# A hybrid attention block on one Trainium2 core: the last inverse softmax sums through TensorE and PSUM, and another order of the first loads

## The chip, the core and the metric

The kernel runs on one core of one Trainium2 chip. The core has five engines that run beside each other, each in the order of its own list of instructions: TensorE (PE) for matmuls, with a row of its own for weight loads (PEld); VectorE (DVE) and ScalarE (ACT) for work on tiles; GpSimd (POOL); and SyncE (SP), which here only issues DMA transfers. ACT and POOL issue transfers too. The metric is the time of one execution on the device in microseconds (us), lower is better.

## What is computed

The reference is one decoder block in float32 with 512 tokens of width 1024. Two attention branches of 8 heads of 64 read the same normalised input through one projection.

```python
h = rms_norm(x, norm_g[layer])
proj = h @ w_in[layer]
fq, fk, fv, fz, mq, mk, mv, mz, ga, gb, fl = split_cols(proj, IN_SPLITS)
...
log_f = jax.nn.log_sigmoid((fl + b_f[layer]).astype(jnp.float32)).transpose(0, 2, 1)
y_fox = from_heads(fox_attention(q, k, v, log_f)) * jax.nn.silu(fz)
...
y_moba = from_heads(moba_attention(q, k, v)) * jax.nn.silu(mz)
merged = (jax.nn.sigmoid(ga + b_gate[layer, 0]) * (y_fox @ w_fox[layer])
          + jax.nn.sigmoid(gb + b_gate[layer, 1]) * (y_moba @ w_moba[layer]))
x = x + merged @ w_out[layer]
```

The first branch (f, "fox") is causal softmax attention with a forget term in its logits. The second (m, "moba") has rotary positions and is causal too; with 512 tokens in blocks of 256 its choice of blocks leaves out nothing. Each softmax divides by a sum over the keys, and this kernel does so at the end of a head, by multiplying the head's output with the inverse of the sum.

## The kernel before, in words

**Precision.** Every matrix is split into a high part and a low part, both of a type that PE takes at its fast pace, and a product is three matmuls: high x high, high x low, low x high. ACT makes the high part by a copy, and DVE makes the low part by a subtraction. For a weight piece this is `split` (L107 to L113: `wh_...` on ACT at L110, `wl_...` on DVE at L112).

**Start.** `load_g` (L96 to L103) loads one of the eight slices of x transposed (`xt`, 256 KB, on SP's queue) and splits it into `Zh` (ACT, L101) and `Zl` (DVE, L102). `load_quarters` (L124 to L139) loads the first weight chunk `fqa` in quarters of two slices. The first quarter comes as two transfers of one slice each, one on ACT's queue and one on SP's, and is split by two casts (L134) and two subtractions (L137), all on DVE. The constants `cs` (L66) go first on ACT's queue. Eight matmuls on zeros (L82) occupy PE at first. `first_qk` (L350 to L361) then runs over the eight slices with four banks of PSUM, three matmuls for each of four token tiles (L358 to L360), 96 in all for `fqa`. The chunks `fka`, `fza`, `fzb` follow; `x_stats` (L197 to L208) makes the inverse norms `r` on POOL behind the rope tables that POOL builds (L329 to L333), `norm_row` (L213 to L217) spreads them over partitions, and `normalise` (L219 to L224) turns xt into the normalised `Gh` and `Gl`. The chunk `fva` and its evictions (L319, L320) are the first users of these.

**Attention.** Four groups of four heads run (`attn_group`, L483 to L633), the last one for branch m, half b. For each head: logits and softmax numerators (L530 to L535), transposes of these into `p_a`, `p_b`, `p_cc` (L576), their split (`pth` on ACT L582, `ptl` on DVE L583), then the products with the values into `pv` (L586, L587) and the assembly of two heads into `ypair` (L611, L612). For each pair of heads, `inverse_sums` (L548 to L550) takes the reciprocals `ri` (tokens on partitions), and `sums_out` (L552 to L558) transposes them on PE, copies them on ACT into `rinv_t` and stores them in DRAM; `sums_in` (L560 to L567) loads them back twice, spread over 64 partitions each (`rinv_bc`, on ACT's queue). `Yp` (L619 to L631) multiplies the silu gate `zs` with `rinv_bc` (L626, on POOL, for the very last pair on DVE), the result with `ypair` (L627), and splits it (`yhm` on ACT L628, `ylm` on DVE L629). Projections and other matmuls are laid between the heads as filler.

**Gates.** The gate projections (`group`, L671 to L770) are computed in seven products of half-size matrices in place of eight. Four products read sums of the input that were stored in DRAM and are loaded back by POOL's queue in `load_sums` (L254 to L258, tiles S0 to S3, high and low). Each product has 24 matmuls (L715 to L718); three of its intermediate results are copied out of PSUM by ACT (`e_GA`, L725). Its weights come through four raw buffers and are split by L110 and L112 as above. `GA0` is the first group behind the last attention group, and `yhm` and `ylm` of the last pair are read only later, by `unit_m` (L775 on).

**What sets the order.** The program is written in the order in which work is wanted, and a scheduler fixes the order on each engine before the run. Dependences are kept by tile: an instruction that reads a tile waits for all its writers. Each engine then runs its list in order, and a waiting instruction holds up those behind it.

Of the kernel before, what the change touches and what calls it, by code (L numbers as in the profile page):

```python
# [7 lines left out]
F32 = mybir.dt.float32  # L8
F32R = mybir.dt.float32r
AF = mybir.ActivationFunctionType  # L10
OP = mybir.AluOpType
AX = mybir.AxisListType

P = 128
S = 512
D = 1024
NT = S // P
KT = D // P
HD = 64
CW = 256  # L20
# [3 lines left out]
WR = 4  # L24
# [5 lines left out]
def fox_moba_kernel(ctx: ExitStack, tc, xT, x, w_in, w_fl, w_fox, w_moba, w_out, cst, rope, out):  # L30


    nc = tc.nc
    V, A, G, T = nc.vector, nc.scalar, nc.gpsimd, nc.tensor

    con = ctx.enter_context(tc.tile_pool(name="con", bufs=1))
    sb = ctx.enter_context(tc.tile_pool(name="sb", bufs=1))
# [3 lines left out]
    stage = {}  # L41

    def enter(name):
        if stage:
            stage.pop("guard").__exit__(None, None, None)
        stage["guard"] = tc.tile_pool(name=name, bufs=1, reuse_waits="tile")
        stage["pool"] = stage["guard"].__enter__()

    def t2(tag, bufs, name, shape=(P, 512), dt=F32):
        pool = stage["pool"] if tag in ("qs", "pt", "pc", "ys") else sb  # L50
        return pool.tile(list(shape), dt, name=name, tag=tag, bufs=bufs)

    def pst(tag, bufs, name):
        return ps.tile([P, 512], F32, name=name, tag=tag, bufs=bufs)
# [4 lines left out]
    def tp(name):  # L59
        return pst("tp", 3, name)  # L60


    cs = con.tile([P, C_END], F32, name="cs")
    rp = con.tile([P, NT, 32], F32, name="rp")
    wfl = con.tile([P, KT, 8], F32, name="wfl")
    nc.scalar.dma_start(out=cs, in_=cst)  # L66

    def col(c, n=1):
        return cs[:, c:c + n]

    ident = con.tile([P, P], F32, name="ident")
    triU = con.tile([P, P], F32, name="triU")
    ones = con.tile([P, P], F32, name="ones")
    mask = con.tile([P, 512], F32, name="mask")
    wsc = t2("u", 4, "wsc", (P, 2))
    V.memset(wsc, 0.0)
    A.activation(wsc, wsc, AF.Square)
# [13 lines left out]

    Gh = con.tile([P, KT, S], F32R, name="Gh")
    Gl = con.tile([P, KT, S], F32R, name="Gl")
    XT, Z = {}, {}

    def load_g(*ks):  # L96
        for k in ks:
            xt = XT[k] = t2("y", 15, f"xt{k}")
            nc.sync.dma_start(out=xt, in_=xT[:, k, :])
            zh, zl = Z[k] = [stage["pool"].tile([P, S], F32R, name=f"Z{hl}{k}") for hl in "hl"]  # L100
            A.activation(zh, xt, AF.Copy, scale=col(C_NG + k))  # L101
            V.scalar_tensor_tensor(zl, xt, col(C_NG + k), zh.bitcast(F32), op0=OP.mult, op1=OP.subtract)  # L102


    chunks = {}
# [15 lines left out]
        V.tensor_tensor(out=lo[:, :, CW:264], in0=f, in1=hi[:, :, CW:264].bitcast(F32), op=OP.subtract)  # L121
        chunks.setdefault(name, []).append((hi, lo))

    def load_quarters(name, c0, hf, between):  # L124
        raw = sb.tile([P, 4, CW], F32, name=f"wr_{name}{hf}", tag="wr", bufs=WR)
        hi = sb.tile([P, 4, 264], F32R, name=f"wh_{name}{hf}", tag="wh", bufs=4)
        lo = sb.tile([P, 4, 264], F32R, name=f"wl_{name}{hf}", tag="wl", bufs=4)
        for q in range(2):
            first = hf == 0 and q == 0
            for k in (slice(0, 1), slice(1, 2)) if first else (slice(2 * q, 2 * q + 2),):  # L130
                (nc.scalar if first and k.start == 0 else nc.sync).dma_start(
                    out=raw[:, k], in_=w_in[c0 // CW, :, 4 * hf + k.start:4 * hf + k.stop, :])
                if first:
                    V.tensor_copy(hi[:, k, :CW], raw[:, k])  # L134
                else:
                    A.activation(hi[:, k, :CW], raw[:, k], AF.Copy)
                V.tensor_tensor(out=lo[:, k, :CW], in0=raw[:, k], in1=hi[:, k, :CW].bitcast(F32), op=OP.subtract)  # L137
            load_g(*between[q])
        chunks.setdefault(name, []).append((hi, lo))  # L139

    COLS = {}
    off = 0
# [50 lines left out]
    r = con.tile([P, NT], F32, name="r")  # L193
# [191 lines left out]
    ZS = {}  # L385
# [94 lines left out]
    ri = con.tile([P, 16, 4], F32, name="rinv")  # L480
    R_dram = dr.tile([16, NT, P], F32, name="r_dram")

    def attn_group(br, half, gq, gk):  # L483
        fox = br == "f"
        qn, kn = QN[f"{br}q{half}"], QN[f"{br}k{half}"]
        hb = 4 * (half == "b") + (0 if fox else 8)
        last = br + half == "mb"
        st = {}
# [63 lines left out]
        def sums_out(pr):  # L552
            h0 = hb + 2 * pr
            p = tp("p_ri")
            T.transpose(p[:8, :P], ri[:, h0:h0 + 2, :].rearrange("p h t -> p (h t)"), ident)
            rt = sb.tile([8, P], F32, name="rinv_t", tag="rinv_t", bufs=1)
            A.activation(rt, p[:8, :P], AF.Copy)
            A.dma_start(out=R_dram[h0:h0 + 2].rearrange("h t p -> (h t) p"), in_=rt)  # L558

        def sums_in(pr):  # L560
            if last and pr:
                rb = st["r", pr] = t2("u", 4, "rinv_bc")
            else:
                rb = st["r", pr] = stage["pool"].tile([P, S], F32, name="rinv_bc", tag="rinv_bc", bufs=1)
            for o in range(2):
                A.dma_start(out=rb[o * HD:(o + 1) * HD, :],
                            in_=R_dram[hb + 2 * pr + o].rearrange("t p -> (t p)").partition_broadcast(HD))  # L567

        def Bb(h):
            def go():  # L570
                pts, vt = st[h], VT[f"{br}v{half}"]
                o = h % 2
                pv = pst("pv", 1, "pv")

                def blk(dst, i, j):
                    T.transpose(dst, pts[i][:, j * P:(j + 1) * P], ident)  # L576

                def spl(p, n):
                    tag, w, bufs = ("pt", 512, 4) if n == 512 else ("pc", 256, 2)
                    hi = t2(tag, bufs, "pth", (P, w), F32R)  # L580
                    lo = t2(tag, bufs, "ptl", (P, w), F32R)
                    A.activation(hi[:, :n], p[:, :n], AF.Copy)  # L582
                    V.tensor_tensor(out=lo[:, :n], in0=p[:, :n], in1=hi[:, :n].bitcast(F32), op=OP.subtract)  # L583
                    return hi, lo
                def pvm(j, hl, c0, n, start, stop):
                    T.matmul(pv[:, P * j:P * j + n], vt[:, j, h, :], hl[0][:, c0:c0 + n], start=start, stop=False)  # L586
                    T.matmul(pv[:, P * j:P * j + n], vt[:, j, h, :], hl[1][:, c0:c0 + n], start=False, stop=stop)  # L587
                pa = tp("p_a")
                for i in range(4):
                    blk(pa[:, i * P:(i + 1) * P], i, 0)  # L590
                pb = tp("p_b")
                for i in range(1, 4):
                    blk(pb[:, (i - 1) * P:i * P], i, 1)
                blk(pb[:, 384:512], 3, 3)
                ha = spl(pa, 512)
                hbb = spl(pb, 512)
                pc = tp("p_cc")
                for i in range(2, 4):
                    blk(pc[:, (i - 2) * P:(i - 1) * P], i, 2)
                hc = spl(pc, 256)  # L600
                pvm(0, ha, 0, 512, True, False)
                pvm(1, hbb, 0, 384, False, False)
                pvm(3, hbb, 384, 128, False, False)
                pvm(2, hc, 0, 256, False, True)
                pr = h // 2
                if o == 0:
                    st["y", pr] = t2("u", 4, "ypair") if last and pr else t2("ys", 1, "ypair")
                y = st["y", pr]
                me, ot = (slice(0, HD), slice(HD, P)) if o == 0 else (slice(HD, P), slice(0, HD))
                sh = t2("u", 4, "ysh")  # L610
                A.activation(sh[me, :], pv[ot, :], AF.Copy)  # L611
                V.tensor_tensor(out=y[me, :], in0=pv[me, :], in1=sh[me, :], op=OP.add)  # L612
                if o == 0:
                    sums_out(pr)
                elif pr:
                    sums_in(1)
            return go

        def Yp(pr):  # L619
            def go():  # L620
                y = st["y", pr]
                gp = 2 * (half == "b") + pr
                yh = t2("y", 15, f"yh{br}{gp}", dt=F32R)
                yl = t2("y", 15, f"yl{br}{gp}", dt=F32R)
                zr = st["r", pr]
                (V if (br, gp) == ("m", 3) else G).tensor_tensor(out=zr, in0=ZS[br, gp], in1=zr, op=OP.mult)  # L626
                V.tensor_tensor(out=y, in0=y, in1=zr, op=OP.mult)  # L627
                A.activation(yh, y, AF.Copy)  # L628
                V.tensor_tensor(out=yl, in0=y, in1=yh.bitcast(F32), op=OP.subtract)  # L629
                Y[br, gp] = (yh, yl)  # L630
            return go  # L631
# [239 lines left out]
        for u in filler(names):  # L871
            u()

    enter("start")
    load_g(0)
    load_quarters("fqa", COLS["fqa"], 0, ((1, 2), (3, 4)))
    load_quarters("fqa", COLS["fqa"], 1, ((5, 6), (7,)))
    nc.sync.dma_start(out=wfl, in_=w_fl)
    load_fl("fka", COLS["fka"], 0)
    load_fl("fka", COLS["fka"], 1)  # L880
# [127 lines left out]
```

## Time and profile before

| quantity | value |
|---|---|
| median of 3 runs | 443.63 us (441.45 to 444.06) |
| the profiled execution | 444.28 us |
| its span, first to last instruction | 442.5 us |
| outside the span | 1.78 us |
| mean granted clock of PE | 0.996 |
| instructions | 8082 |
| DMA in all | 56.40 MB, mean 127 GB/s |

The profile is of one execution. Busy time of an engine is the time in which it has an instruction that works; PE's matmuls overlap, so that the time of one is longer than the step from one to the next. A row of the timeline gives start, length, engine, line and operation, and in brackets the idle time before it with what ended it. A chain is followed back from the last instruction, each step to what released it. The costliest groups of the page that lie near the change, with busy time, mean duration in ns and the idle time before:

```profile
L112 DVE TENSOR_TENSOR wl_GA<-wr_ga,wh_GA 128x1024 fp32r<-128x1024 f32 x14 | 16.6, 1219 | 1.2 <-ACT wh_GA L110 1.1
L110 ACT ACTIVATE wh_GA<-wr_ga 128x1024 fp32r<-128x1024 f32 x14 | 14.5, 1054 | 4.5 <-DVE wr_ga L679 2.7
...
L583 DVE TENSOR_TENSOR ptl<-p_a,pth 128x512 fp32r<-128x512 f32 x16 | 11.0, 687 | 5.1 <-ACT pth L582 5.0
```

### The profile page before, as it was taken

The page shows a single profiled execution, that of the slowest core. Times are in us where ns is not written, and L with a number is a line of the kernel's source. Part 1 is how long each engine was busy: PE and PEld are TensorE (multiplying, and loading weights), DVE is VectorE, ACT ScalarE, POOL GpSimd, SP SyncE. Part 2 cuts the span into 40 slices and gives each one's busy share as a digit, 9 for nine tenths or more (in the row PEclk, how much of TensorE's full clock was granted, in tenths as well). Part 3 has the DMA queues.
Part 4 walks back from the last instruction along what each step waited for, and adds up shares of the span by engine and source line. Part 5 has one row for each costly group of instructions (what it writes and reads, how often), then busy time and mean ns, then how long its engine had stood idle before and what let it go on. Part 6 is the DMA issues. An engine that isn't in the chain of part 4 may idle for free.

```text
span 442.5 us, 8082 instructions
## 1 busy us (share of the span) xinstructions
PE 428.4 (97%) x3100; PEld 403.9 (91%) x3100; DVE 314.7 (71%) x563; ACT 262.5 (59%) x491; POOL 87.6 (20%) x106
## 2 busy tenths in 40 slices
PE   6999999999999999999999999987999999999996
PEld 5998899999999998899998878877999989989996
DVE  5559994777998869676956689928978786584311
ACT  5676544876777769887765876717655545531100
POOL 1059200224142950134621002200000000000000
PEclk9999999999999999999999999998999999999999
DMA  8962164424377413303304212663134405624231
GB/s 261 388 246 69 54 205 137 111 74 136 110 233 209 103 55 120 119 13 122 106 14 132 95 24 90 232 203 96 60 133 126 160 1 183 197 96 152 88 96 48
DMA packets 25991, 56.40 MB, mean 127 GB/s; under 512 B 3296, under 2 KB 11936, under 8 KB 25952
## 3 DMA queue, kind: packets, MB, share of 16 engines
q1 hardware_dynamic: 14528, 39.95, 27.4%
q10 hardware_dynamic: 10272, 11.74, 9.0%
q0 software_dynamic: 1152, 4.19, 2.8%
q8 instruction: 24, 0.39, 0.4%
q14 instruction: 15, 0.12, 0.1%
HBM read 46.27 MB, written 6.32 MB: 119 GB/s over the span
## 4 chain that ended last, share of the span: by engine, by line
PE 85%; ACT 6%; DMA 4%; DVE 2%; issue 1%; ACTq 0%; SPq 0%; DVEq 0%
PE pb_GB L718 3%; PE pb_GB L717 3%; PE pb_GB L715 3%; PE po L815 3%; PE po L817 3%; PE po L816 3%; PE pb_GA L715 2%; PE pb_GA L717 2%; PE pb_GA L718 2%; PE pv L587 2%; PE pv L586 2%; PE lg L530 2%; PE lg L531 2%; PE pm L644 2%; PE pm L645 2%; PE pm L646 2%
## 5 line engine op out<-in xcount | busy, mean ns | idle before, releaser
L535 ACT ACTIVATE p<-p,negm 128x128 f32<-128x128 f32 (+1 forms) x64 | 35.7, 558 | 12.5 <-DVE negm L533 11.2
L310 POOL TENSOR_TENSOR ff<-ss,mh 128x8 f32<-128x8 f32 x16 | 27.1, 1699 | 79.6 <-DVE ss L308 77.3
L533 DVE CUSTOM_DVE_ANT_0 p<-lg,mask 128x128 f32<-128x128 f32 (+1 forms) x64 | 30.5, 485 | 5.8 <-PE lg L531 5.6
L815 PE MATMUL po<-wh_wo,mgh 128*128 128x256 f32 x96 | 27.1, 282 | 0.0
L817 PE MATMUL po<-wh_wo,mgl 128*128 128x256 f32 x96 | 27.0, 282 | 0.0
L816 PE MATMUL po<-wl_wo,mgh 128*128 128x256 f32 x96 | 26.9, 281 | 0.0
L825 DVE TENSOR_TENSOR ot<-po,xr 128x256 f32<-128x256 f32 x16 | 6.6, 424 | 24.7 <-PE po L817 23.6
L110 ACT ACTIVATE wh_wo<-wr_wo 128x1024 fp32r<-128x1024 f32 x8 | 8.5, 1061 | 21.6 <-PE po L817 8.0
L530 PE MATMUL lg<-KH,QS 128*128 128x128 f32 (+1 forms) x64 | 20.7, 332 | 0.4 <-DMA KH<-KH 0.4
L112 DVE TENSOR_TENSOR wl_GB<-wr_gb,wh_GB 128x1024 fp32r<-128x1024 f32 x14 | 16.8, 1223 | 4.2 <-ACT wh_GB L110 3.3
L110 ACT ACTIVATE wh_GB<-wr_gb 128x1024 fp32r<-128x1024 f32 x14 | 14.6, 1059 | 8.6 <-PE pm L645 2.5
L612 DVE TENSOR_TENSOR ypair<-pv,ysh 64x512 f32<-64x512 f32 x16 | 11.0, 688 | 10.8 <-ACT ysh L611 10.7
L816 PEld LDWEIGHTS po<-wl_wo,mgh 128*128 128x128 f32 x96 | 18.1, 189 | 0.0
L815 PEld LDWEIGHTS po<-wh_wo,mgh 128*128 128x128 f32 x96 | 18.1, 189 | 0.0
L817 PEld LDWEIGHTS po<-wh_wo,mgl 128*128 128x128 f32 x96 | 18.1, 188 | 0.0
L715 PE MATMUL pb_GA<-Gh,wh_GA 128*128 128x256 f32 x48 | 14.3, 298 | 3.3 <-ACT e_GA L725 3.3
L112 DVE TENSOR_TENSOR wl_GA<-wr_ga,wh_GA 128x1024 fp32r<-128x1024 f32 x14 | 16.6, 1219 | 1.2 <-ACT wh_GA L110 1.1
L110 ACT ACTIVATE wh_GA<-wr_ga 128x1024 fp32r<-128x1024 f32 x14 | 14.5, 1054 | 4.5 <-DVE wr_ga L679 2.7
L504 DVE SCALAR_TENSOR_TENSOR QS<-p_qT,cs,QS 64x512 fp32r<-64x512 f32 x16 | 12.0, 750 | 6.6 <-ACT QS L503 6.2
L611 ACT ACTIVATE ysh<-pv 64x512 f32<-64x512 f32 x16 | 9.5, 593 | 9.8 <-PE pv L587 8.0
L112 DVE TENSOR_TENSOR wl_wo<-wr_wo,wh_wo 128x1024 fp32r<-128x1024 f32 x8 | 9.8, 1222 | 7.4 <-ACT wh_wo L110 7.4
L583 DVE TENSOR_TENSOR ptl<-p_a,pth 128x512 fp32r<-128x512 f32 x16 | 11.0, 687 | 5.1 <-ACT pth L582 5.0
(448 smaller groups left out, 1798.8 us busy)
## 6 DMA issues: line engine op xcount, KB each, us to landing
wr_ga<-in_w_in_dram SPq DMA_DIRECT2D x8, 512.0 KB
wr_gb<-in_w_in_dram SPq DMA_DIRECT2D x8, 512.0 KB
wr_wo<-in_w_out_dram SPq DMA_DIRECT2D x8, 512.0 KB
xt<-in_xT_dram SPq DMA_DIRECT2D x8, 256.0 KB
x<-in_x_dram SPq DMA_DIRECT2D x8, 256.0 KB
s_dramh<-sum_sh ACTq DMA_DIRECT2D x8, 256.0 KB
s_draml<-sum_sl ACTq DMA_DIRECT2D x8, 256.0 KB
KH<-KH ACTq DMA_DIRECT2D x16, 128.0 KB
```

Of the source, the lines that this page charges most:

```text
L110: A.activation(hi[:, :, 0:n], src, AF.Copy)
L112: eng.tensor_tensor(out=lo[:, q, 0:n], in0=src[:, q], in1=hi[:, q, 0:n].bitcast(F32), op=OP.subtract)
L310: G.tensor_tensor(out=f2, in0=ss.rearrange("p t h -> p (t h)"), in1=mh, op=OP.pow)
L530: T.matmul(lg[:, :n], qs[:, qt], kh[:, :n], start=True, stop=False)
L533: V.tensor_tensor_reduce(pt, lg[:, :n], mask[:, 512 - n:512], -0.125, 3.0e38, op0=OP.add, op1=OP.min, accum_out=mkn[:, hh, i:i + 1])
L535: A.activation(pt, pt, AF.Exp, bias=mkn[:, hh, i:i + 1], scale=-1.0, accum_out=rs[:, hh, i:i + 1])
L715: T.matmul(o, hi[:, k, cc], lh, start=(n < 3 and c == 0 and k == 0), stop=False, skip_group_check=True)
L717: T.matmul(o, hi[:, k, cc], ll, start=False, stop=False, skip_group_check=True)
L718: T.matmul(o, lo[:, k, cc], lh, start=False, stop=(k == 3), skip_group_check=True)
L815: T.matmul(p[:, :CW], gh[:, st], hi[:, k, :CW], start=(kk == 0), stop=False)
L816: T.matmul(p[:, :CW], gh[:, st], lo[:, k, :CW], start=False, stop=False)
L817: T.matmul(p[:, :CW], gl[:, st], hi[:, k, :CW], start=False, stop=(kk == KT - 1))
```

## The change

**First loads.** All loads of xt and of `fqa` are issued at the very start by one function. ACT's queue gets xt0 and then cs. SP's queue gets the first two weight slices in one transfer of 256 KB, then xt1, slices 2 and 3 (256 KB), xt2, xt3, slices 4 to 7 (512 KB), xt4 to xt7. `load_g` becomes `split_x` and `load_quarters` becomes `first_split`, which only split. The first quarter is now cast by one instruction of 512 elements a partition, and has one subtraction.

```diff
+    def first_loads():
+        def xt(eng, k):
+            XT[k] = t2("y", 15, f"xt{k}")
+            eng.dma_start(out=XT[k], in_=xT[:, k, :])
+
+        def w(k0, k1):
...
+            nc.sync.dma_start(out=RAW[hf][:, k0 - 4 * hf:k1 - 4 * hf], in_=w_in[0, :, k0:k1, :])
+        xt(nc.scalar, 0)
+        w(0, 2)
+        nc.scalar.dma_start(out=cs, in_=cst)
+        xt(nc.sync, 1)
+        w(2, 4)
+        xt(nc.sync, 2)
+        xt(nc.sync, 3)
+        w(4, 8)
+        for k in range(4, KT):
+            xt(nc.sync, k)
...
+    def first_split(hf, between):
...
         for q in range(2):
...
+            k = slice(2 * q, 2 * q + 2)
+            if hf == 0 and q == 0:
+                V.tensor_copy(hi[:, k, :CW], raw[:, k])
+            else:
+                A.activation(hi[:, k, :CW], raw[:, k], AF.Copy)
+            V.tensor_tensor(out=lo[:, k, :CW], in0=raw[:, k], in1=hi[:, k, :CW].bitcast(F32), op=OP.subtract)
+            split_x(*between[q])
```

**Last inverse sums.** For the very last pair of heads the way through DRAM is left out. POOL writes `ri` into a tile `rinv_w` in which each token's value stands 64 times for each of the two heads, PE transposes it in four steps into a PSUM tile `p_rinv`, and DVE multiplies the gate `zs` with it from there. The other pairs keep their way.

```diff
         def sums_in(pr):
             if last and pr:
-                rb = st["r", pr] = t2("u", 4, "rinv_bc")
...
+                return
...
-                if o == 0:
+                if o == 0 and not (last and pr):
                     sums_out(pr)
...
-                zr = st["r", pr]
-                (V if (br, gp) == ("m", 3) else G).tensor_tensor(out=zr, in0=ZS[br, gp], in1=zr, op=OP.mult)
+                if last and pr:
+                    zr, rb = ZS[br, gp], pst("lg", 2, "p_rinv")
+                    h0 = hb + 2 * pr
+                    rw = t2("u", 4, "rinv_w")
+                    for o in range(2):
+                        G.tensor_copy(rw.rearrange("p (t o d) -> p t o d", o=2, d=HD)[:, :, o, :],
+                                      ri[:, h0 + o, :, None].to_broadcast([P, NT, HD]))
+                    for t in range(NT):
+                        T.transpose(rb[:, t * P:(t + 1) * P], rw[:, t * P:(t + 1) * P], ident)
+                    V.tensor_tensor(out=zr, in0=zr, in1=rb, op=OP.mult)
+                else:
+                    zr = st["r", pr]
+                    G.tensor_tensor(out=zr, in0=ZS[br, gp], in1=zr, op=OP.mult)
                 V.tensor_tensor(out=y, in0=y, in1=zr, op=OP.mult)
```

**The order that the scheduler makes of it.** PE's number of matmuls for `fqa` stays, but for the first slice the products with `Zl` come after the others. In the last attention group, three transposes of the last head's p_a move ahead of the pv group of the head before, p_b and p_cc come right behind that group, and 13 matmuls of GA stand between them and the last pv group. The four transposes into p_rinv stand after 19 of the 24 matmuls of GA's fourth product. On ACT, two wh_GA, e_GA, wh_GA and e_GA now come ahead of yhm; on DVE, zs x p_rinv and the second ypair come behind two wl_GA. POOL makes rinv_w behind the issue of its last S load.

More of the change, by code (lines that the diff above doesn't have):

```diff
@@ L60, in tp @@
         return pst("tp", 3, name)
+    XT, RAW = {}, {}
+    def first_loads():
[3 more added lines that the diff above has]
+        def w(k0, k1):
+            hf = k0 // 4
+            if hf not in RAW:
+                RAW[hf] = sb.tile([P, 4, CW], F32, name=f"wr_fqa{hf}", tag="wr", bufs=WR)
+            nc.sync.dma_start(out=RAW[hf][:, k0 - 4 * hf:k1 - 4 * hf], in_=w_in[0, :, k0:k1, :])
[9 more added lines that the diff above has]
+            xt(nc.sync, k)
     cs = con.tile([P, C_END], F32, name="cs")
@@ L65, in fox_moba_kernel @@
     wfl = con.tile([P, KT, 8], F32, name="wfl")
-    nc.scalar.dma_start(out=cs, in_=cst)
     def col(c, n=1):
@@ L74, in fox_moba_kernel @@
     mask = con.tile([P, 512], F32, name="mask")
+    enter("start")
+    first_loads()
     wsc = t2("u", 4, "wsc", (P, 2))
@@ L93, in fox_moba_kernel, with split_x @@
     Gl = con.tile([P, KT, S], F32R, name="Gl")
-    XT, Z = {}, {}
-    def load_g(*ks):
+    Z = {}
+    def split_x(*ks):
         for k in ks:
-            xt = XT[k] = t2("y", 15, f"xt{k}")
-            nc.sync.dma_start(out=xt, in_=xT[:, k, :])
+            xt = XT[k]
             zh, zl = Z[k] = [stage["pool"].tile([P, S], F32R, name=f"Z{hl}{k}") for hl in "hl"]
@@ L122, in load_fl @@
         chunks.setdefault(name, []).append((hi, lo))
[L124 to L127, printed above, removed]
+    def first_split(hf, between):
+        raw = RAW[hf]
+        hi = sb.tile([P, 4, 264], F32R, name=f"wh_fqa{hf}", tag="wh", bufs=4)
+        lo = sb.tile([P, 4, 264], F32R, name=f"wl_fqa{hf}", tag="wl", bufs=4)
         for q in range(2):
[L129 to L139, printed above, removed]
+            k = slice(2 * q, 2 * q + 2)
[5 more added lines that the diff above has]
+            split_x(*between[q])
+        chunks.setdefault("fqa", []).append((hi, lo))
     COLS = {}
@@ L561, in sums_in @@
             if last and pr:
-                rb = st["r", pr] = t2("u", 4, "rinv_bc")
-            else:
-                rb = st["r", pr] = stage["pool"].tile([P, S], F32, name="rinv_bc", tag="rinv_bc", bufs=1)
+                return
+            rb = st["r", pr] = stage["pool"].tile([P, S], F32, name="rinv_bc", tag="rinv_bc", bufs=1)
             for o in range(2):
@@ L872, in seq @@
             u()
[L874 to L877, printed above, removed]
+    split_x(0)
+    first_split(0, ((1, 2), (3, 4)))
+    first_split(1, ((5, 6), (7,)))
     nc.sync.dma_start(out=wfl, in_=w_fl)
```

## The prediction, made before the changed kernel ran

> **What bounds the kernel now.** I read the page's busy times first, then its chain, then the waits and the chain around the stretches in which TensorE (PE) stands still.
>
> ```profile
> PE 428.4 (97%) x3100; PEld 403.9 (91%) x3100; DVE 314.7 (71%) x563; ACT 262.5 (59%) x491; POOL 87.6 (20%) x106
> ...
> PE 85%; ACT 6%; DMA 4%; DVE 2%; issue 1%; ACTq 0%; SPq 0%; DVEq 0%
> ```
>
> PE is busy 428.4 of the 442.5 us span and makes up 85% of the chain. No other engine comes near, so a change pays only where PE idles (14.1 us in all), where PE runs at a lower clock, or where PE gets fewer instructions. The two parts of this change sit at two such places: the start, and the end of the last attention group.
>
> The waits between 285 and 302 us, and the chain there (start, length, what):
>
> ```profile
> DVE rinv_bc L626 <- DMA rinv_bc<-r_dram: 6.0, 1, 6.0
> PEld pb_GA L715 <- ACT e_GA L725: 3.5, 1, 3.5
> PE pb_GA L715 <- ACT e_GA L725: 3.3, 1, 3.3
> ...
> PE pv L587 <- DVE ptl L583: 0.9, 1, 0.9
> ```
> ```profile
> 289.65 6.68 DMA rinv_bc<-r_dram
> 296.42 0.70 DVE rinv_bc L626
> 297.15 0.70 DVE ypair L627
> 297.99 0.42 issue
> 298.41 1.99 ACT wh_GA L110 x2
> 300.40 0.49 ACT e_GA L725
> 300.93 0.58 PE pb_GA L715
> ```
>
> PE never uses the inverse sums in this stretch, yet it waits for them. The broadcast from DRAM takes 6.68 us; VectorE (DVE) and then ScalarE (ACT) stand behind it in their own order, and two weight copies and the eviction e_GA, which PE does need, are queued on ACT behind the stalled yhm. PE resumes at 300.93, 3.3 us late.
>
> The same chain at PE's restart and at the start of the kernel, by stretches (from:to, length, then busy time and count of PE, PEld, DVE, ACT, POOL; clock; DMA share; GB/s):
>
> ```profile
> 8.00:13.80 5.80, 5.80 (x28) 5.80 (x28) 5.80 (x10) 4.77 (x9) 0.00 (x0) 1.00 1.03 365
> 13.80:18.00 4.20, 4.20 (x38) 4.20 (x37) 2.66 (x6) 3.49 (x7) 0.00 (x0) 1.00 1.04 399
> 39.48:61.87 22.39, 22.39 (x122) 19.17 (x120) 22.39 (x39) 12.73 (x18) 7.67 (x10) 1.00 0.22 72
> 301.00:304.00 3.00, 3.00 (x14) 3.00 (x15) 2.97 (x4) 2.60 (x3) 0.00 (x0) 0.51 0.53 158
> ```
>
> At the start 28 matmuls take 5.80 us (0.207 each), then 38 take 4.20 (0.111). The clock column reads 1.00 in both, so there I trust the spacing. After the stall 14 matmuls take 3.00 us (0.214) at clock 0.51, the slow one of the two paces. So the stall costs its 3.3 us and a slow stretch behind it.
>
> **Part 1, the first loads.** PE's first matmul, DVE's first rows with one later split, ACT's first split, and the DMA that the chain names:
>
> ```profile
> 7.74 1.19 PE L358 MATMUL fqa<-wh_fqa,Zh 128*128 128x256 f32 x4 [2.41 <-DVE wh_fqa L134]
> ```
> ```profile
> 5.97 0.29 DVE L134 CAST wh_fqa<-wr_fqa 128x256 fp32r<-128x256 f32 x1 [4.46 <-DMA wr_fqa<-in_w_in_dram]
> 6.30 0.42 DVE L137 TENSOR_TENSOR wl_fqa<-wr_fqa,wh_fqa 128x256 fp32r<-128x256 f32 x1
> 6.64 0.74 DVE L102 SCALAR_TENSOR_TENSOR Zl<-xt,cs,Zh 128x512 fp32r<-128x512 f32 x1
> 7.31 0.28 DVE L134 CAST wh_fqa<-wr_fqa 128x256 fp32r<-128x256 f32 x1
> ...
> 9.29 0.68 DVE L137 TENSOR_TENSOR wl_fqa<-wr_fqa,wh_fqa 128x512 fp32r<-128x512 f32 x1
> ```
> ```profile
> 4.27 0.72 ACT L101 ACTIVATE Zh<-xt,cs 128x512 fp32r<-128x512 f32 x1 [1.52 <-DMA cs<-in_cst_dram]
> ```
> ```profile
> 1.24 4.71 DMA wr_fqa<-in_w_in_dram
> ```
>
> PE stands idle for 2.41 us, up to 7.74, because it waits for the second cast, which DVE runs only after wl and Zl. Both casts write one tile, so the first matmul needs both. The change removes one cast and one wl (four instructions of 256 become two of 512) and puts the first 256 KB of weights at the head of SP's queue; xt1 no longer stands between its halves. The weights landed at 1.24 + 4.71 = 5.95. The bytes that must be there (xt0, cs, two slices of w) are the same as before. I take 5.5: not before 4.6, since cs and xt0 are in at 4.27 and 256 KB follow; not after 6.3, if the single large piece completes as a whole and later. The joint cast is about 0.5 (twice 0.29 less one fixed part), then 0.15 to PE as in 7.31 + 0.28 to 7.74: first matmul near 6.2. The second one needs wl (0.68), so it runs near 6.85, and from there PE is fed (per slice of the weights DVE needs 0.74 + 0.34 = 1.1 us, PE 12 matmuls, 1.3 at full pace). One matmul of 0.21 is done ahead of that, so PE is effectively 7.74 - 6.85 + 0.21 = 1.1 us earlier, between 0.3 (landing at 6.3) and 2.0 (4.6).
>
> The clock adds to this. PE ran slow from 7.74 to 13.8 (6.1 us), but for only 3.0 us after the stall at 301. If the slow part of the start shrinks to 3.0, the 3.1 us won are run at 0.111 in place of 0.207 per matmul, which saves 3.1 x 0.46 = 1.4. [...] So the raw gain lies between 1.1 and 2.5.
>
> Can the next stage take it? Waits of DVE from 31.9 to 39.6 us, then POOL's rows, then the last DVE row that holds PE:
>
> ```profile
> DVE xf L291 <- ACT qn_fka L289: 1.1, 1, 1.1
> DVE xt L221 <- ACT rbc L217: 0.3, 1, 0.3
> DVE wl_fzb L112 <- ACT wh_fzb L110: 0.3, 1, 0.3
> ```
> ```profile
> 26.97 0.67 POOL L329 TENSOR_TENSOR tab_mq<-rp,cs 128x64 f32<-128x64 f32 x1 [24.63 <-DMA rp<-in_rope_dram]
> ...
> 30.77 1.04 POOL L208 TENSOR_TENSOR r<-mm,mh 128x4 f32<-128x4 f32 x1
> ```
> ```profile
> 61.46 0.41 DVE L320 TENSOR_TENSOR v_fva<-pj_fva,v_fva 128x256 fp32r<-128x256 f32 x1
> ```
>
> DVE is full from 39.48 to 61.87 (22.39 of 22.39), and PE's third group of fva needs the bank that the row at 61.46 frees. That chain starts with r on POOL, which queues behind the rope tables and so behind the landing of rp at 26.97, a transfer limited by bytes (399 GB/s). If r stays at 31.8, DVE can only save what it idled behind it, 1.1 + 0.3 + 0.3 = 1.7. If rp lands earlier, or the tables (26.97 to 30.77) run faster on POOL, the whole raw gain can pass, at most 2.0 + 1.4 = 3.4. I take **G1 = 1.8**, by the nearest number, 1.7, and inside the raw 1.1 to 2.5; its ends are 0.3 and 3.4.
>
> **Part 2, the last inverse sums.** Removed: one transpose (p_ri), one ACT copy, one store to DRAM and two broadcast loads. Added: two POOL copies (rinv_w), four transposes (p_rinv) after 19 of the 24 matmuls of the fourth product, and a DVE multiply that reads PSUM in place of SBUF. In the new static order e_GA on ACT no longer stands behind yhm, which comes after it. What goes: the 3.3 us wait and the slow stretch, 14 x (0.214 - 0.111) = 1.4; together 4.7. Late next is e_GA itself: the two copies of 1.99 us and its own 0.49 start when the third product ends, and are done 2.6 us later with releases, while PE has 24 x 0.111 + 0.44 (four transposes, row below) = 3.1 us to run. That leaves 0.5 us in hand.
>
> The order also changes in front of it. The pv group of the last head, alone (columns as above), against the one before it, then four transposes in the chain:
>
> ```profile
> 282.29:283.72 1.43, 1.43 (x8) 1.14 (x8) 0.00 (x0) 0.00 (x0) 1.00 0.45 183
> 285.85:289.08 3.23, 2.24 (x8) 1.23 (x8) 0.00 (x0) 0.00 (x0) 1.00 0.79 250
> ```
> ```profile
> 275.16 0.44 PE p_a L576 x4
> ```
>
> The last group takes 3.23 where 1.43 would do, as its ptl sits behind a wl_GA of DVE. In the new order p_b and p_cc are made earlier and 13 matmuls of GA stand between them and pv. I expect 0.3 to 0.4 of the 1.8 to remain: 1.4 gained (0 to 1.8). The four transposes cost 0.44 less the one of p_ri, a quarter of that: 0.3. **G2 = 4.7 + 1.4 - 0.3 = 5.8**, ends 4.3 (no gain at pv) and 6.2.
>
> POOL's copies have no row of their own kind. Near ones, by form (busy, mean ns, idle):
>
> ```profile
> L626 POOL TENSOR_TENSOR rinv_bc<-zs_mzb,rinv_bc 128x512 f32<-128x512 f32 x1 | 1.6, 1599 | 28.4 <-DMA rinv_bc<-r_dram 28.4
> L329 POOL TENSOR_TENSOR tab_mk<-rp,cs 128x64 f32<-128x64 f32 x1 | 1.4, 1384 | 0.0
> ```
>
> Each copies 256 elements a partition: by the first row 0.8 us, by the slowest (1384 ns for 64) 5.5. POOL is free after its last S load is issued near 287.4, so they are ready by 289 and at worst by 298.4. PE comes to p_rinv near 295.3. I cost them at nothing; without that cover it is up to 3.1 us. What the DVE multiply costs in PSUM lies off PE's path.
>
> **Sum.** 444.28 (the profiled execution, 442.5 of span and 1.78 around it) - 1.8 - 5.8 = **436.7**. The median, 443.63, lies 0.65 below that execution, which I leave for the range.
>
> **The rivals.**
> A, the start gives almost nothing: the queues share one bandwidth, the weights land at 5.95 again, the second matmul runs at 5.95 + 0.5 + 0.15 + 0.68 = 7.3, PE is 7.74 - 7.3 + 0.21 = 0.6 us earlier, and the slow stretch ends where it did. For it: DMA is full (379 to 399 GB/s by then, share over 1.0) and POOL's r may not move. Against: xt1's share of the traffic is gone. 444.28 - 0.6 - 5.8 = 437.9. [...] Chance 0.18.
> B, another wait takes half of the stall's place: the 0.5 us in hand is an estimate out of sums; if ACT's copies come 2 us later, PE stops again, 1.5 us, and the slow stretch of 1.4 comes back. 444.28 - 1.8 - 2.9 = 439.6. Chance 0.14.
> C, the other side: PE runs in order, and all its matmuls stand behind p_rinv. If POOL's two copies were ready only after 303 (over 7.7 us each, more than the slowest row's 5.5), PE would lose 295.3 to 303 and a slow stretch, 7.7 + 1.4 = 9.1, more than 1.8 + 5.8 + 1.4: 444.28 - 1.8 - 5.8 + 9.1 = 445.8. Nothing in the profile comes near that. Chance 0.04.
>
> **How the numbers follow.** The forecast has 0.64. About 1% (439.2 to 448.1 around the median) is what a measurement here can tell from no change. Forecast and A end below 439.2 with most of their spread, and B straddles it: faster 0.78, same 0.18, slower 0.04. The range goes from 444.28 - 3.4 - 6.2 = 434.7, less the 0.65 of the median, to B with a weaker start (444.28 - 0.8 - 2.9): 434.0 to 440.6.
>
> **What would show it.** Right: first fqa matmul near 6.2; full pace from about 10.5; no wait of pb_GA on e_GA near 295; the last pv group under 2 us; no half clock around 300. Wrong: first matmul after 7; a stop at p_rinv or e_GA; fva waiting for DVE near 60 with more than 1 us, which would eat the start; or a new half-clock stretch in the gates.

## The result and the profile after

The changed kernel takes 439.23 us (median of six runs); the kernel before, run beside it, takes 443.85. The ratio is 0.9876, with a 95% interval of 0.9846 to 0.9907: a gain of 1.2%, with an interval that stays clear of 1. One of the six runs, 463.88, ran at a mean clock of 0.85 and is left out of that ratio and of the spread, 437.97 to 439.47 (without it the median is 439.03). The profiled execution took 438.43, its span 436.7; before it was 444.28 and 442.5. The forecast was 436.7, in a range of 434.0 to 440.6.

From the page of the profile of the changed kernel, its span, its busy times and the shares of its chain:

```profile
span 436.7 us, 8081 instructions
...
PE 425.6 (97%) x3103; PEld 401.5 (92%) x3103; DVE 316.0 (72%) x561; ACT 262.1 (60%) x490; POOL 89.5 (20%) x108
...
PE 84%; DVE 6%; ACT 5%; DMA 3%; issue 1%; ACTq 0%; DVEq 0%
```

DMA and ACT lost share in the chain, and DVE gained. Where the time went is told by how far PE has come at three places. The first rows are of the kernel before, the second of the changed one: the last group of matmuls (by kind, with the start of the first and of the last one) of the first chunk, of fva, and of the gates GA.

```profile
L360 PE MATMUL fqa<-wh_fqa,Zl x32: 277/281/415, 8.9 to 21.7; 128*128 128x256 f32 x32
...
L284 PE MATMUL pj_fva<-wh_fva,Gl x32: 274/281/283, 56.5 to 67.8; 128*128 128x256 f32 x32
...
L715 PE MATMUL pb_GA<-S2h,wh_GA x16: 276/281/287, 305.5 to 327.9; 128*128 128x256 f32 x16
```
```profile
L380 PE MATMUL fqa<-wh_fqa,Zl x32: 276/280/415, 9.8 to 21.2; 128*128 128x256 f32 x32
...
L304 PE MATMUL pj_fva<-wh_fva,Gl x32: 274/280/364, 55.9 to 67.8; 128*128 128x256 f32 x32
...
L745 PE MATMUL pb_GA<-S2h,wh_GA x16: 276/280/287, 299.6 to 322.0; 128*128 128x256 f32 x16
```

At the end of fva both kernels stand at 67.8: in this pair of profiles the new loads gave nothing. At the end of GA the changed one is 5.9 us ahead, and this is the difference of the spans (5.8). So the gain came from the end of attention alone.

There, the stretches of the changed kernel (columns as in the prediction), the last pv group by itself, and the new instructions:

```profile
290.00:297.00 7.00, 7.00 (x62) 7.00 (x61) 3.93 (x5) 2.90 (x4) 0.00 (x0) 1.00 0.65 231
297.00:301.00 4.00, 4.00 (x36) 4.00 (x35) 3.80 (x5) 3.05 (x4) 0.00 (x0) 1.00 0.37 125
301.00:304.00 3.00, 3.00 (x27) 3.00 (x27) 2.83 (x4) 2.61 (x4) 0.00 (x0) 1.00 0.03 8
```
```profile
285.95:287.76 1.81, 1.71 (x8) 1.15 (x8) 0.00 (x0) 0.00 (x0) 1.00 0.87 274
```
```profile
287.25 1.75 POOL L649 COPY rinv_w<-rinv 128x256 f32<-128x256 f32 x2
```
```profile
293.35 1.06 ACT L133 ACTIVATE wh_GA<-wr_ga 128x1024 fp32r<-128x1024 f32 x1 [1.66 <-PE pb_GA L747]
294.32 0.58 ACT L755 ACTIVATE e_GA<-pb_GA 128x512 f32<-128x512 f32 x1
```

PE is full from 290 to 304 and at full clock; from 301 to 304 it now does 27 matmuls in place of 14. The last pv group takes 1.81 in place of 3.23. POOL's two copies take 1.75 together (0.41 and 1.40 by their own records) and are done at 289.0, well ahead of the four transposes at 295.5. The e_GA that PE waited for before ends at 294.9.

At the start, the first rows of PE, DVE and ACT, and the transfer that the chain names:

```profile
8.38 0.39 PE L378 MATMUL fqa<-wh_fqa,Zh 128*128 128x256 f32 x1 [3.04 <-ACT Zh L124]
```
```profile
6.47 0.43 DVE L154 CAST wh_fqa<-wr_fqa 128x512 fp32r<-128x512 f32 x1 [4.95 <-DMA wr_fqa<-in_w_in_dram]
6.93 0.69 DVE L157 TENSOR_TENSOR wl_fqa<-wr_fqa,wh_fqa 128x512 fp32r<-128x512 f32 x1
```
```profile
7.61 1.34 ACT L124 ACTIVATE Zh<-xt,cs 128x512 fp32r<-128x512 f32 x2 [4.38 <-DMA cs<-in_cst_dram]
```
```profile
1.26 6.26 DMA cs<-in_cst_dram
```

The first matmul comes 0.64 later than before, not 1.5 earlier, and so the prediction's own sign of being wrong, "first matmul after 7", came true. It waits for the first split of x, and that waits for the constants cs. They are 34 KB, but come second on ACT's queue behind xt0, and landed at 7.52; before, they were first there and in by 4.27. The profiles of the experiments agree: with these loads the first matmul came at 7.80 and 8.09, each time behind the wait of ACT for cs, and with the old loads at 7.38 to 7.51.

### The profile page after: what moved, and what is told of

Its sections match the earlier page's. It is cut to its first block, busy times and chain, and to the rows that moved or that the text cites. A ratio compares the mean times of both kernels' runs of the same rounds, so it can differ in the third digit from the quotient of the medians.

```text
span 436.7 us, 8081 instructions
## 1 busy us (share of the span) xinstructions
PE 425.6 (97%) x3103; PEld 401.5 (92%) x3103; DVE 316.0 (72%) x561; ACT 262.1 (60%) x490; POOL 89.5 (20%) x108
## 4 chain that ended last, share of the span: by engine, by line
PE 84%; DVE 6%; ACT 5%; DMA 3%; issue 1%; ACTq 0%; DVEq 0%
PE pb_GB L748 3%; PE pb_GA L748 3%; PE pb_GB L747 3%; PE pb_GA L745 3%; PE pb_GB L745 3%; PE pb_GA L747 3%; PE po L845 3%; PE po L847 3%; PE po L846 3%; PE pv L606 2%; PE pv L605 2%; PE lg L550 2%; PE lg L551 2%; PE pm L674 2%; PE pm L675 2%; PE pm L676 2%
## 5 line engine op out<-in xcount | busy, mean ns | idle before, releaser
L528 DVE SCALAR_TENSOR_TENSOR KL<-p_kT,cs,KH 64x512 fp32r<-64x512 f32 x16 | 12.0, 749 | 2.4 <-ACT KH L526 2.1
L748 PE MATMUL pb_GA<-Gh,wl_GA 128*128 128x256 f32 x48 | 13.6, 283 | 0.0
```

The costliest lines, as they stand in the source:

```text
L748: T.matmul(o, lo[:, k, cc], lh, start=False, stop=(k == 3), skip_group_check=True)
```

## The experiments

Each kernel ran in five rounds beside the kernel before, which took 443.85 beside the first five changed kernels of the table, 444.09 beside the next four and 443.51 beside the last two. The ratios go by these, over all runs, and differ by up to 0.002 from the ratios of the medians. "First matmul" is that of fqa, "fqa" and "fva" the start of the last matmul with the low part of x (Zl, Gl), all from one profile of each kernel; spread is lowest to highest run.

| kernel | first matmul | fqa | fva | median us | spread | ratio to before, 95% interval |
|---|---|---|---|---|---|---|
| before (the profile shown) | 7.74 | 21.7 | 67.8 | 443.85 | 440.9 to 446.1 | 1 |
| changed | 8.38 | 21.2 | 67.8 | 439.23 | 437.97 to 439.47 | 0.9876, 0.9846 to 0.9907 |
| sums only | 7.38 | 18.7 | 64.8 | 437.97 | 436.02 to 439.04 | 0.9851, 0.9822 to 0.9881 |
| loads only | 7.80 | 21.9 | 68.5 | 444.49 | 442.01 to 446.67 | 1.0012, 0.9985 to 1.0039 |
| constants first on ACT's queue | 8.95 | 22.2 | 68.8 | 439.44 | 439.14 to 440.53 | 0.9891, 0.9866 to 0.9915 |
| last pair on POOL | 7.44 | 18.8 | 65.5 | 438.95 | 436.92 to 439.46 | 0.9883, 0.9854 to 0.9911 |
| changed, 16 zeros | 8.09 | 19.3 | 65.4 | 436.34 | 435.54 to 437.41 | 0.9823, 0.9797 to 0.9848 |
| constants alone on ACT's queue, 12 zeros | 6.54 | 18.7 | 65.2 | 435.94 | 435.70 to 436.09 | 0.9810, 0.9786 to 0.9834 |
| sums only, 12 zeros | 7.51 | 18.8 | 66.3 | 437.26 | 436.63 to 437.79 | 0.9840, 0.9817 to 0.9863 |
| constants alone on ACT's queue | 6.43 | 19.8 | 66.4 | 436.40 | 436.22 to 436.56 | 0.9821, 0.9797 to 0.9845 |
| the first of these, gates on POOL | 6.51 | 19.1 | 70.3 | 440.62 | 437.63 to 442.04 | 0.9932, 0.9903 to 0.9960 |
| constants alone, small pieces | 6.57 | 18.4 | 66.1 | 437.13 | 436.07 to 438.13 | 0.9874, 0.9836 to 0.9911 |

("The first of these" is the kernel with the constants alone on ACT's queue and 12 zeros.)

**Each part by itself.** The kernel before with the four edits of the sums, and the kernel before with the edits of the loads.

> The kernel before with the second part alone: the last inverse sums through PSUM, the first loads as they were. Theory 1 (the whole gain comes from the sums, the new loads give nothing): about as fast as the changed kernel, 443.9 - 5.5 = 438.4, within 0.7 of it. Rival (as predicted, the new loads are worth 1.8 us): slower than the changed kernel by 1.8, about 441.

> The kernel before with the first part alone: the new first loads, the last inverse sums through DRAM as before. Theory 1: the same as before, 443.9 within 0.7; the constants, now second on their queue, land near 7.5, the first matmul runs near 8.4, and the 3.3 us wait at the end of attention stays. Rival: 1.8 us faster than before, 442.

The sums alone save 5.9 us (443.85 to 437.97); the loads alone change nothing (443.85 to 444.49, the interval includes 1). The rival, 1.8 us from the loads, falls. In the profile of the loads alone the constants landed at 6.94 and the first matmul ran at 7.80, both a little earlier than expected and both later than in the profiles of the old loads. The loads-only kernel keeps both old waits at the end of attention:

```profile
PE pb_GA L735 <- ACT e_GA L745: 3.0, 1, 3.0
PE pv L607 <- DVE ptl L603: 0.9, 1, 0.9
```

The table holds a surprise: "sums only" has the start of the kernel before, instruction for instruction, yet its fqa ends 3 us earlier. One row each, of the sums-only kernel and the changed one, for the stretch of which the prediction showed 28 matmuls before:

```profile
8.00:13.80 5.80, 5.80 (x51) 1.00 1.00 345
```
```profile
8.00:13.80 5.80, 5.42 (x33) 0.71 1.02 375
```

51 matmuls in place of 28 in the same 5.8 us (columns: PE alone, clock, DMA share, GB/s): with the same start code PE ran at full pace from the first matmul in the sums-only execution, and at half pace in that of the kernel before. The clock column reads 1.00 in both, so this is told by the spacing, 0.114 and 0.207 us. The changed kernel, with 33, lies between: its clock column reads 0.71. Of the 3.0 us at the end of fqa, 0.4 is the earlier first matmul and 2.6 is the pace. So the same code starts up to 3 us faster or slower, most of it by PE's pace, and single profiles can't be compared for the start.

**The constants ahead of the first slice of x.**

```diff
+        nc.scalar.dma_start(out=cs, in_=cst)
         xt(nc.scalar, 0)
         w(0, 2)
-        nc.scalar.dma_start(out=cs, in_=cst)
```

> The changed kernel with the constants ahead of the first slice of x on ACT's queue, nothing else changed. Theory 1a (the late constants hold the first split and so the first matmul): constants land near 4.4, and the first matmul comes by 7.2 in place of 8.4. Theory 1b (VectorE, full from 39 to 61 us, sets the time there): the won us is gone when fva ends, and the whole time is within 0.6 of the changed kernel's. Rival to 1a: the weights or the first slice of x are late too, first matmul at 8 or later. Rival to 1b: the time drops by 1 us or more.

The first matmul came at 8.95, later still, and the time is that of the changed kernel. The rival to 1a came true, because of the order on ACT that the scheduler made of it:

```profile
7.57 0.63 ACT L156 ACTIVATE wh_fqa<-wr_fqa 128x512 fp32r<-128x512 f32 x1 [4.34 <-DMA wr_fqa<-in_w_in_dram]
8.17 1.98 ACT L124 ACTIVATE Zh<-xt,cs 128x512 fp32r<-128x512 f32 x3
```

The split of the second piece of weights now stands ahead of the first split of x and holds it until 8.17. The run therefore doesn't tell by itself what the constants cost, nor does it test 1b; the kernel with the constants alone on the queue does the first.

**The waiting work moved to POOL, the way through DRAM kept.**

```diff
-                (V if (br, gp) == ("m", 3) else G).tensor_tensor(out=zr, in0=ZS[br, gp], in1=zr, op=OP.mult)
-                V.tensor_tensor(out=y, in0=y, in1=zr, op=OP.mult)
-                A.activation(yh, y, AF.Copy)
-                V.tensor_tensor(out=yl, in0=y, in1=yh.bitcast(F32), op=OP.subtract)
+                G.tensor_tensor(out=zr, in0=ZS[br, gp], in1=zr, op=OP.mult)
+                W = G if last and pr else V
+                W.tensor_tensor(out=y, in0=y, in1=zr, op=OP.mult)
...
+                    G.tensor_copy(yh, y)
...
+                W.tensor_tensor(out=yl, in0=y, in1=yh.bitcast(F32), op=OP.subtract)
```

> The kernel before, where for the last pair all four steps behind the inverse sums (the two multiplies, the high copy, the low part) run on POOL; the way through DRAM and the old order of the last pv group stay. Theory (the stall is a matter of what stands in line behind the waiting instruction on VectorE and ScalarE, not of the way through DRAM): the 3.3 us wait of PE on e_GA and the slow stretch go, 4.7 us, while the last pv group still takes 3.2 us; 443.9 - 4.7 = 439.2. Rival (the way through DRAM costs by itself, by its transfers or because something else needs its result soon): less than 2 us faster, 442 or more.

438.95 against an expected 439.2. PE's only wait in this stretch is the one of the last pv group; POOL has the long one, and there only the other steps of the same pair stand behind it:

```profile
PE pv L587 <- DVE ptl L583: 0.9, 1, 0.9
```
```profile
294.10 1.65 POOL L626 TENSOR_TENSOR rinv_bc<-zs_mzb,rinv_bc 128x512 f32<-128x512 f32 x1 [9.11 <-DMA rinv_bc<-r_dram]
295.82 1.29 POOL L628 TENSOR_TENSOR ypair<-ypair,rinv_bc 128x512 f32<-128x512 f32 x1
```

Across the stretch (PE's first to last matmul of GA, 280.62 to 333.87 before, 278.22 to 326.54 here) this kernel gains 4.9 us, the changed one 6.0. So the way through DRAM cost nothing by being slow; it cost because its waiters stood in DVE's and ACT's lines. The rest, 1.1, is what the forecast had for the shorter pv group less the transposes (1.4 less 0.3).

**Longer zeros, and the constants alone on ACT's queue.** "12 zeros" and "16 zeros" are `WARM` at 12 and 16 in place of 8. The loads of the other two:

```diff
-        xt(nc.scalar, 0)
+        nc.scalar.dma_start(out=cs, in_=cst)
+        xt(nc.sync, 0)
         w(0, 2)
-        nc.scalar.dma_start(out=cs, in_=cst)
```

> The changed kernel with 16 in place of 8 matmuls on zeros at the start, nothing else changed. Theory 2 (at the start the granted clock decides, and it opens late because PE idles 2 to 3.6 us between the zeros and the first real matmul): the zeros now end near the first real matmul, the full pace holds from then on in every run, fqa ends by 19 to 20 in place of 21.5 to 22.5, and the time drops by about 2 to 437.2 with a smaller spread. Rival (loads and VectorE set the time of the start): first matmul and end of fqa move by less than 0.7 us, time 439.2 within 0.7; or slower, if the zeros run past 8.4.

> The kernel with the sums alone (first loads as before) and 12 matmuls on zeros. Theory 2: fqa ends near 19.0 in every run, as it did in the profile of the kernel with the sums alone, where the clock was full from 6.0 on; time near that kernel's fastest runs, 436.2, with a spread under 1.5 us. Rival (the clock at the start is not what spreads the runs): 438.0, spread 3 us as before.

> As the kernel with constants alone on ACT's queue and the first slice of x at the head of SP's queue, with 8 matmuls on zeros as in the changed kernel. Theory 3 (the new loads lost because the constants came second on a queue): first matmul by 6.8 in place of 8.4, time 1 to 1.5 below the changed kernel, 438.0, still with a spread of 2 to 3 us from the clock. Rival (the same bytes have to land whatever the order): first matmul near 7.5 as before, no faster than the kernel with the sums alone.

> The changed kernel with the constants alone on ACT's queue, the first slice of x at the head of SP's queue ahead of the first weights, and 12 matmuls on zeros. Theory 2 and theory 3 (what must land first is what is issued first; two slices of weights behind one of x land by 5.9 and one joint cast follows): first matmul by 6.8, full pace from the start, fqa ends by 18.5; time 435.5 to 436.5. Rival (VectorE, full from 39 to 61 us, takes the won time back): fqa ends early, but fva ends no earlier than in the kernel with the sums alone, time 437.5 or more.

With 16 zeros and the loads unchanged, fqa ends at 19.3 and the median falls by 2.9, to 436.34 (by 3.1 against the kernel before in each case; the two intervals barely touch). The first matmul moves by only 0.3 (8.09) and the end of fqa by 1.9, so most of this start is PE's pace: 51 matmuls between 8.0 and 13.8 in place of 33, at a clock column of 1.00 in place of 0.71. The expected smaller spread did not come (1.9 us; the row of the changed kernel has 1.5). With 12 zeros on the old loads fqa ended at 18.8 and the spread fell to 1.2, as expected, but the time did not: the median, 437.26, is 1.2 us above the fastest run of the kernel without them and only 0.7 below its median, with intervals that overlap. In its profile PE waited at fva, which sums-only did not:

```profile
PE pj_fva L282 <- DVE v_fva L320: 1.0, 1, 1.0
```

With the constants alone on ACT's queue and 8 zeros:

```profile
6.43 0.98 PE L378 MATMUL fqa<-wh_fqa,Zh 128*128 128x256 f32 x3 [1.10 <-DVE wh_fqa L154]
```
```profile
5.86 0.43 DVE L154 CAST wh_fqa<-wr_fqa 128x512 fp32r<-128x512 f32 x1 [4.34 <-DMA wr_fqa<-in_w_in_dram]
6.20 0.75 DVE L125 SCALAR_TENSOR_TENSOR Zl<-xt,cs,Zh 128x512 fp32r<-128x512 f32 x1
6.87 0.68 DVE L157 TENSOR_TENSOR wl_fqa<-wr_fqa,wh_fqa 128x512 fp32r<-128x512 f32 x1
```

The first matmul comes at 6.43, so theory 3 holds, and 436.40 is 1.6 better than expected; the expected spread of 2 to 3 us did not come (0.34). Constants first on ACT's queue and the first slice of x first on SP's, the weights still land by 5.86, as they did at 5.95 before: here the order on the queues decided what was late, not how soon all three were in. Against sums-only this kernel is 1.6 us faster by the medians, close to the 1.8 that the prediction gave the loads. But the intervals overlap, and the fastest run of sums-only, 436.02, is as fast, so what the loads are worth in this order is not settled. With 12 zeros added the kernel takes 435.94, inside the expected 435.5 to 436.5, and has the lowest median here: 0.9810 of the kernel before. In its profile fqa ends at 18.7 and fva at 65.2, no earlier than the 64.8 of sums-only; that half of the rival came true, its time of 437.5 did not.

**Two that settle little.**

> As the kernel with the constants alone on ACT's queue and 12 matmuls on zeros, and with the four multiplies of the fox gates (zs by its sigmoid, 0.68 us each on VectorE) moved to POOL. Theory 4 (what still takes back time behind the start is VectorE, busy without a break from 39 to 61 us, so that PE waits for an eviction of fva): the eviction of the first fva bank comes about 2 us earlier, the 0.4 us that PE lost there go, time 435.5. Rival (POOL's slower copies of the same multiply delay the gates' users or slow VectorE): 436 or slower.

Slower, 440.62. The multiplies ran on POOL, but the scheduler also put the running sums of the forget gates further ahead in PE's list (at 62.2, with fva ending at 70.3; without the move at 64.2 and 65.2), and PE stood behind them:

```profile
PE p_c L470 <- DVE fg L464: 2.9, 1, 2.9
```

So theory 4 was not tested; the run shows only that this move, with the order that came of it, costs more than it could save.

> As the kernel with the constants alone on ACT's queue and 8 matmuls on zeros (first matmul at 6.43, 436.4), but with the weights of the first chunk in smaller pieces: one slice for each of the first four, two for each of the last four, in place of 2, 2 and 4; three transfers more on SP's queue, 0.4 us of issue each. If the size of the pieces matters: first matmul 0.4 or more later, time 0.4 or more higher. If the queue only needs enough bytes in flight: first matmul within 0.3, time within 0.4 of it.

The first matmul is within 0.14 of the large pieces' (6.57 and 6.43), so in this profile the size of the pieces didn't matter for what the change meant it for. The median is 0.7 higher, more than the 0.4 named, but PE waited 1.5 for the eviction of fva there against 0.3, and the spreads overlap; whether the pieces caused that stays open.

## Why the prediction was right, and where it was wrong

- **The total** was right in range and sign: 436.7 forecast, 439.23 measured, a gain of 4.6 where 7 to 7.6 was forecast. It is right by one part of two: with the loads at nothing the same sum gives 444.28 - 5.8 = 438.5, and the profiled execution took 438.43. The range reached far enough for that because it had room for a weak start.
- **Part 2, 5.8, held, and so did its terms.** Measured 6.0 in the profiles and 5.9 between the medians of sums-only and before. The stall and the slow stretch: 4.7 forecast, 4.9 in the kernel with the last pair on POOL. The last pv group: 0.3 to 0.4 forecast to remain, 1.81 less 1.43 measured. POOL's copies: 0.8 each forecast, 1.75 together measured, and hidden. (The lower end of G2, 4.3, should be 4.7 - 0.3 = 4.4; nothing hangs on it.)
- **The slack of e_GA** was put at 0.5. The sum had two weight copies start behind the third product; one of them ran earlier, at 290.64. So e_GA ended at 294.9, the product that needs it begins at 296.6, and the slack was about 1.7. Rival B was further off than its chance of 0.14 said.
- **Part 1, 1.8, failed.** The step was "The bytes that must be there (xt0, cs, two slices of w) are the same as before. I take 5.5": the sum followed the weights alone. The change also moved cs from the head of ACT's queue to behind xt0, and that move was never costed, although cs stood among the bytes that must be there. It landed at 7.52, 1.6 after the weights of before. The weights themselves came at 6.45 in that profile, outside the 4.6 to 6.3 that was allowed for them, but at 5.6 and 5.8 in two others with the same loads; cs was the later one in all three. With cs at the head again and xt0 on SP's queue, the first matmul came at 6.43, near the forecast 6.2, so the rest of the step (landing, joint cast) was sound.
- **Rival A** came nearest to what happened at the start (437.9 forecast), by another way: not the weights but the constants were late. That the queues share one bandwidth was its supposition. The rows fit it but don't tell one queue from another: between 8.0 and 13.8 the DMA share is 1.00 to 1.03, at 345 to 375 GB/s, in the rows shown, of the old and of the new order of loads. How soon one piece lands did depend on the order and on the execution: the first weights were in between 5.6 and 6.5 in three orders, and at 4.59 with the constants ahead of xt0 on ACT's queue, where the next weights, on which ACT waited, came only at 7.54.
- **The clock's term, 1.4, was too small and not tied to the change.** The same start code ran fqa to 21.7 in one execution and to 18.7 in another, 2.6 of it by the pace. That the slow part of the start could shrink to the 3.0 us measured behind the stall was my estimate. In the profile of the kernel before it lasted 6.1 us, and in that of sums-only, with the same start code, there was none (28 and 51 matmuls in the same 5.8 us); no row shows what decides between the two. I had used the pace for a gain and not for the spread.
- **The cap by DVE, 1.7,** was too low. Sums-only carried 3.0 of 3.0 us from fqa past fva. The prediction had named the way: "If rp lands earlier, or the tables (26.97 to 30.77) run faster on POOL, the whole raw gain can pass". In sums-only rp landed as before (27.00), but the tables ran faster, and r began at 29.07 in place of 30.77:

```profile
28.38 0.31 POOL L329 TENSOR_TENSOR tab_mk<-rp,cs 128x64 f32<-128x64 f32 x1
29.07 1.05 POOL L208 TENSOR_TENSOR r<-mm,mh 128x4 f32<-128x4 f32 x1
```

The first of these took 1.38 before. DVE's wait of 1.1 for qn_fka went too, and the normalisation of xt, with which its full stretch begins, started at 36.43 in place of 39.48. Why POOL is slower in one execution than in another is open. In other kernels 0.3 to 1.5 us were lost to a wait for v_fva, and what decides that was not found either.

## What to carry to other kernels

Here a slow transfer, 6.68 us long, cost by what was queued in order behind the instruction that waited for it: the kernel that kept it and moved the waiting work won 4.9 us, of the 6.0 that the changed kernel won there. Follow each engine's line past the waiter before pricing the transfer. When a load is moved, price every transfer that it is moved ahead of, the small ones that all the work needs above all (the constants, 34 KB, landed at 7.52 in place of 4.27). And keep TensorE busy, on zeros if need be, until the first real matmul can run: more zeros took 2.9, 0.7 and 0.5 us off the median in three pairs of kernels, and in the first and the last of these no run of the one overlaps a run of the other.

## What the runs showed of the hardware that was not expected

The pace of PE at the start, for the same code, moved the end of fqa by 2.6 us (21.7 or 18.7, less the 0.4 of the first matmul), more than either order of loads did. With eight matmuls on zeros, three of eight profiles had the full pace from the first real matmul on. How long PE idled behind the zeros does not sort them: the full pace came after 2.04, 2.11 and 1.24 us, the half pace after 2.41, 2.47 and 3.61, but also after 1.10, with the constants alone on ACT's queue; after 3.04, in the changed kernel, the full pace lasted for some four matmuls and then halved. With 12 or 16 zeros, behind which PE idled for at most 1.1 us, all four profiles had the full pace. There the zeros themselves had sped up before their end: eight took 3.78 us, twelve 4.59 to 4.84 and sixteen 6.70, where the pace of the first eight would have given 5.7 and 7.6.
